# A pinned first tile with zero products beside it, and token sums moved into attention

## The chip, the cores and the metric

The kernel runs on one core of a Trainium2 chip. The metric is the device time of one execution in microseconds (us). The engines are TensorE (PE in the profile; its weight loads are PEld), VectorE (DVE), ScalarE (ACT), GpSimd (POOL) and SyncE (SP), which issues most of the loads.

## The reference

One decoder layer on 512 tokens behind 16 learned meta tokens, D = 1024, all in float32:

```python
h  = concat(meta_tokens, x)                    # 528 x 1024
hn = rmsnorm(h, norm_mix_pre)
rq, rk, rv, rg, sq, sk, sv, ga, gb = split(hn @ w_in)
y_ret = (silu(rg) * groupnorm(retention(rotary(rq), rotary(rk), rv))) @ w_ret_out   # 4 heads, dk 256, dv 512
y_sb  = stick_breaking(sq, sk, sv) @ w_sb_out                                      # 16 heads of 64
mix   = (sigmoid(ga) * y_ret + sigmoid(gb) * y_sb) @ w_out
h = h + rmsnorm(mix, norm_mix_post)
a, b = split(rmsnorm(h, norm_ffn_pre) @ w_ffn_in)                                  # 2816 each
h = h + rmsnorm((silu(a) * b) @ w_ffn_out, norm_ffn_post)
return h[16:]
```

## The kernel before

**Products in two parts.** Every float32 operand of a large product is split: ACT copies it to a rounded hi part (`wh`, `hT`, `th`), and VectorE subtracts that from the value for a lo part (`wl`, `hL`, `tl`); `split` and `lo_of` do this, at L104 and L101. A product is three passes, hi by hi, hi by lo and lo by hi (`mm`, L95). Transposes through TensorE are `turned`, L98.

**Weights** come as blocks of up to 1 MB into `raw` (two buffers), and are split into units of 1024 columns a partition (`wh`, `wl`, five buffers of each). A raw buffer is loaded again when its units are split, and a unit is written again when its products are done.

**Order.** The program is planned when it is built: a planner with a timeline of its own costs places the instructions of each engine, and may move an instruction past others where nothing forbids it. `keep_in_program_order` pins an instruction among the pinned ones. While `pinned[0]` is set, in attention and in the last products, all of PE's instructions are pinned. At run time each engine executes its queue in order.

**The stages that matter here, in order.**

1. The start. The gain `norm_mix_pre` (`grow`) is transposed and spread over a PSUM tile `gps`. The five tiles of the sequence (four of 128 tokens, `x0` to `x3`, and the meta tokens) are loaded, normalised (`innorm`: sum of squares on ACT at L666, the factor by `rstd_of` on VectorE and a power on POOL at L148, the scaled `hx` on VectorE at L671), transposed and split into `hT` and `hL`. Meanwhile the values of attention's first eight heads are formed (`Values(0)` and `Values(1)`, one weight block each, `part(j)` for token tile j), and then the first Q and K (`qk_work`), whose results take banks of `bank_p`, a pool of two.
2. Attention, eight pairs of heads. For each head, `head` lists scores (`z`: two sigmoids on ACT, a scan and a product on VectorE), transposes (`t`), the meta tokens' weights (`tm`, with copies on POOL) and the products with the values (`pv`); projections of the next pairs and of the branch gates fill in between as `Work` items.
3. The output projection of attention with `w_sb_out`, eight feature products of 5.6 us each.
4. Retention, head by head, beginning with `rv_proj(0)`: these projections use a seven-product scheme on quarters (`seven`, `tok_seven`), which needs sums of quarters of the weights (POOL, `tok_quarters`, L233 to L236 for the first block and L244 later) and of the tokens (`Tokens`: four sums for each of four feature tiles k, kept as `th` and `tl`).
5. The merge, the output projection, the FFN, and the last norm.

**Token sums.** `Tokens.row_steps(k, t, u)` is a generator. For one feature tile it issues ten pinned POOL operations of 256 columns (L175) into the four sums `t` with `u` as scratch, then a copy of all four to `th` on ACT (L184) and four pinned POOL subtractions into `tl`. Stage 3 calls it for all four tiles, eight steps beside each feature product:

```python
for _ in range(8):
    next(token_sums, None)
```

**The end.** For each token tile, two halves c of the last product are followed by a square with its sum on ACT (L1249), a product with the gain on VectorE (L1250), then the factor (`rs`, VectorE L1252 and a power on POOL L1253) and the last line on VectorE (L1256), whose result is stored.

Of the kernel before, what the change touches and what calls it, by code (L numbers as in the profile page):

```python
# [10 lines left out]
F32 = mybir.dt.float32  # L11
# [23 lines left out]
def hybrid_block(  # L35
# [64 lines left out]
    def lo_of(lo, src, hi):  # L100
        nc.vector.tensor_tensor(lo, src, hi.bitcast(F32), op=ALU.subtract)  # L101
# [51 lines left out]
    class Tokens:  # L153
# [15 lines left out]
        def row_steps(self, k, t, u):  # L169

            b11, b12, b21, b22 = [[v[:, k, :].bitcast(F32) for v in self.quarter(i, j)] for i in range(2) for j in range(2)]
            t1, t2, t3, t4 = [t[:, n, :] for n in range(4)]

            def op(d, p, q, o):
                tc.keep_in_program_order(nc.gpsimd.tensor_tensor(d, p, q, op=o))  # L175
# [8 lines left out]
            nc.scalar.activation(self.th[:, :, k, :], t, AF.Copy)  # L184
            for n in range(4):
                yield op(self.tl[:, n, k, :], t[:, n, :], self.th[:, n, k, :].bitcast(F32), ALU.subtract)
# [210 lines left out]
    with tc.tile_pool(name="s2", bufs=2, side=RS, reuse_waits="tile") as s2:  # L397
# [29 lines left out]
        class Values:  # L427
# [10 lines left out]

            def part(self, js):
# [47 lines left out]
        def qk_work(work, p, what="qk"):  # L487
# [3 lines left out]
            def q_steps(us):  # L491
                ps = bank_p()
# [12 lines left out]
            def k_steps(us):  # L505
# [3 lines left out]
                for i in range(2):  # L509
                    cs = slice(264 * i, 264 * (i + 1))  # L510
                    pk = bank_p()[:, :264]
# [118 lines left out]

        def tm(p, hd, j):
            turn_meta(hd, metas[p][hd])

# [25 lines left out]

        def innorm(i):  # L660
            n = NM if i == NT else P
            c0 = 0 if i == NT else NM + i * P
            xt = xts[i]
            junk = bank_a().rearrange("p a b -> p (a b)")
            ss = cst.tile([P, 1], F32, name=f"ss{i}")
            nc.scalar.activation(junk[:n], xt[:n], AF.Square, accum_out=ss[:n])  # L666
            rstd_of(ss[:n], ss[:n], 1e-6, 1.0 / D, n)
# [10 lines left out]
        nc.sync.dma_start(grow, g_mix_pre.rearrange("o (k p) -> (o k) p", p=P))  # L678
        xload(0)

        pg = bank_b()
        turned(pg[:, :KD], grow, ident[:KD, :KD])
        nc.scalar.activation(gcol, pg[:, :KD], AF.Copy)
        for k in range(KD):
            turned(gps[:, k // 4, (k % 4) * P : (k % 4 + 1) * P], gcol[:, k : k + 1].to_broadcast([P, P]), ident)
        vals = [Values(0), Values(1)]
        innorm(0)
        vals[0].load()
        xload(1)
# [82 lines left out]
    with tc.tile_pool(name="s3", bufs=1, side=RS, reuse_waits="tile") as s3:  # L772
        s3.tile([P, 2, T], F32, tag="gb", name="gb", bufs=2)

        def all_rows():
            for k in range(KH):
                t = s3.tile([P, 4, H], F32, tag="ts", name="ts", bufs=2)
                yield from tokens.row_steps(k, t, s3.tile([P, H], F32, tag="tu", name="tu", bufs=2))

        token_sums = all_rows()  # L780
# [12 lines left out]
        for f in range(0, KD, 2):  # L793
# [4 lines left out]
            for e in range(2):  # L798
# [4 lines left out]
                for _ in range(8):  # L803
                    next(token_sums, None)
# [398 lines left out]
    with tc.tile_pool(name="s8", bufs=2, side=RS, reuse_waits="tile") as s8:  # L1203
# [38 lines left out]
        for i in range(NT):  # L1242
            sc, fo = [col("sc0"), col("sc1")], s8.tile([P, D], F32, tag="fo", name="fo")
            for c in range(2):
# [4 lines left out]
                nc.scalar.activation(sq, banks[i][c], AF.Square, scale=D**-0.5, accum_out=sc[c])  # L1249
                nc.vector.tensor_tensor(fo[:, cs], banks[i][c], gfin[:, cs], op=ALU.mult)  # L1250
            rs = col("rs")
            nc.vector.scalar_tensor_tensor(rs, sc[0], 1e-6, sc[1], op0=ALU.add, op1=ALU.add)  # L1252
            nc.gpsimd.tensor_tensor(rs, rs, nhalf, op=ALU.pow)  # L1253
# [47 lines left out]
```

## Time and profile before

| | us |
|---|---|
| median of 3 runs | 1198.09 (1197.95 to 1198.48) |
| the profiled execution, its own time | 1197.83 |
| its span, first to last instruction | 1196.0 |
| TensorE busy | 1168.3 (98%) |
| VectorE busy | 851.2 (71%) |
| ScalarE busy | 529.8 (44%) |
| GpSimd busy | 348.7 (29%) |

In the rows of the profile, `out<-in` names the tiles of an instruction, a bracket at the end of a row tells how long its engine stood idle before it and what ended that, and L with a number is a line of the kernel. Rows of the timeline begin with the start and the duration in us; "x2" merges neighbouring instructions of a kind. Ends of products are modelled and overlap; the pitch from one start to the next is their rate.

### The profile page before, as it was taken

How to read it: one execution, taken by the hardware profiler on the slowest of the kernel's cores; microseconds unless marked ns; L12 is line 12 of the kernel's file. 1: busy time of each engine (PE TensorE's matmuls, PEld its weight loads, DVE VectorE, ACT ScalarE, POOL GpSimd, SP SyncE). 2: the span in 40 equal slices, each digit the busy share in tenths (PEclk: the TensorE clock that was granted, in tenths of full speed). 3: DMA queues.
4: the chain of work that ended last, by engine and by line, in shares of the span. 5: the costliest groups of instructions: out<-in, count | busy, mean ns of one | idle time of the engine just before them, and what ended most of it. 6: DMA issues, size and time to landing. Idle time of an engine off the chain costs nothing.

```text
span 1196.0 us, 18637 instructions
## 1 busy us (share of the span) xinstructions
PE 1168.3 (98%) x7521; PEld 1058.4 (88%) x7521; DVE 851.2 (71%) x1120; ACT 529.8 (44%) x899; POOL 348.7 (29%) x374
## 2 busy tenths in 40 slices
PE   7999999999999999999999999999999999999997
PEld 7988999988888988988898898788999999998886
DVE  5588788887447865687577657776799999983333
ACT  5476676666223434334243424344354444443321
POOL 2011122125864401340341120001366666620000
PEclk9999999999999999999999999999999999999999
DMA  6222222233532224122222414334132333253311
GB/s 196 84 85 89 63 64 73 75 99 110 190 116 71 81 71 141 36 81 100 78 73 79 141 54 141 132 135 139 44 106 81 114 98 130 84 185 106 103 39 71
DMA packets 98055, 118.24 MB, mean 99 GB/s; under 512 B 2584, under 2 KB 74272, under 8 KB 97968
## 3 DMA queue, kind: packets, MB, share of 16 engines
q1 hardware_dynamic: 97536, 115.98, 30.0%
q8 instruction: 59, 0.97, 0.3%
q10 hardware_dynamic: 432, 1.07, 0.3%
q14 instruction: 28, 0.23, 0.1%
HBM read 109.96 MB, written 7.08 MB: 98 GB/s over the span
## 4 chain that ended last, share of the span: by engine, by line
PE 76%; DVE 9%; POOL 6%; issue 4%; ACT 2%; DMA 2%; DVEq 0%; POOLq 0%; SPq 0%; ACTq 0%
PE pp L95 34%; PE pb L95 17%; PE pa L95 15%; PE pc L95 5%; DVE wl L101 3%; PE px L95 3%; PE pb L98 3%; DMA raw<-in_w_in_dram 2%; POOL ts L175 2%; POOL tl L175 2%; ACT wh L104 1%; DVE sm L574 1%; POOL raw L244 1%; POOL st L244 1%; DVE ub L266 1%
## 5 line engine op out<-in xcount | busy, mean ns | idle before, releaser
L101 DVE TENSOR_TENSOR wl<-raw,wh 128x1024 fp32r<-128x1024 f32 x196 | 265.9, 1363 | 79.5 <-ACT wh L104 76.1
L104 ACT ACTIVATE wh<-raw 128x1024 fp32r<-128x1024 f32 x196 | 196.9, 1013 | 209.0 <-PE pa L95 78.0
L95 PE MATMUL pp<-hT,wh 128*128 128x512 f32 (+1 forms) x320 | 116.5, 364 | 1.3 <-DVE qb L101 1.1
L95 PE MATMUL pp<-hL,wh 128*128 128x512 f32 (+1 forms) x320 | 112.3, 351 | 0.0
L95 PE MATMUL pp<-hT,wl 128*128 128x512 f32 (+1 forms) x320 | 112.1, 350 | 0.0
L101 DVE TENSOR_TENSOR wl<-st,wh 128x1024 fp32r<-128x1024 f32 x54 | 84.8, 1575 | 15.6 <-ACT wh L104 15.5
L244 POOL TENSOR_TENSOR st<-raw 128x512 f32<-128x512 f32 x28 | 43.6, 1579 | 159.8 <-DMA raw<-in_w_in_dram 159.8
L95 PE MATMUL pp<-qk,wh 128*128 128x512 f32 x256 | 83.2, 399 | 2.0 <-ACT qk L104 1.7
L95 PE MATMUL pp<-wh,hT 128*128 128x256 f32 (+1 forms) x240 | 75.0, 313 | 0.7 <-ACT hT L104 0.7
L95 PE MATMUL pp<-wh,hL 128*128 128x256 f32 (+1 forms) x240 | 74.4, 310 | 0.8 <-DVE ss L147 0.8
L95 PE MATMUL pp<-wl,hT 128*128 128x256 f32 (+1 forms) x240 | 73.9, 308 | 0.0
L104 ACT ACTIVATE wh<-st 128x1024 fp32r<-128x1024 f32 x54 | 56.0, 1055 | 35.5 <-POOL st L244 17.2
L95 PEld LDWEIGHTS pp<-hT,wl 128*128 128x128 f32 x320 | 60.2, 188 | 8.3
L584 POOL CAST mg<-sp 128x32 fp32r<-128x32 f32 x32 | 7.4, 230 | 204.5 <-DVE sp L575 155.1
L95 PEld LDWEIGHTS pp<-hT,wh 128*128 128x128 f32 x320 | 60.2, 188 | 7.5 <-issue 1.3
L95 PE MATMUL pa<-hT,wh 128*128 128x264 f32 (+1 forms) x192 | 62.4, 325 | 2.8 <-DVE rt L891 2.8
L95 PEld LDWEIGHTS pp<-hL,wh 128*128 128x128 f32 x320 | 60.4, 189 | 5.3
L574 DVE TENSOR_TENSOR_SCAN sm<-sm,mask 128x528 f32<-128x528 f32 (+1 forms) x64 | 54.9, 858 | 12.5 <-ACT sm L571 11.6
L148 POOL TENSOR_TENSOR rs<-rs,nhalf 128x1 f32<-128x1 f32 x20 | 12.7, 636 | 170.7 <-DVE rs L147 170.7
L95 PE MATMUL pa<-hL,wh 128*128 128x264 f32 (+1 forms) x192 | 62.2, 324 | 0.0
L95 PE MATMUL pa<-hT,wl 128*128 128x264 f32 (+1 forms) x192 | 62.1, 324 | 0.0
L95 PEld LDWEIGHTS pp<-qk,wh 128*128 128x128 f32 x256 | 47.6, 188 | 13.4 <-ACT qk L104 2.4
(326 smaller groups left out, 3726.8 us busy)
## 6 DMA issues: line engine op xcount, KB each, us to landing
raw<-in_w_in_dram SPq DMA_DIRECT2D x28, 1024.0 KB, 5.0
raw<-in_w_ffn_in_dram SPq DMA_DIRECT2D x22, 1024.0 KB, 5.1
raw<-in_w_in_dram SPq DMA_DIRECT2D x32, 512.0 KB, 4.2
raw<-in_w_ffn_out_dram SPq DMA_DIRECT2D x11, 1024.0 KB, 4.9
raw<-in_w_ret_out_dram SPq DMA_DIRECT2D x8, 1024.0 KB, 5.0
raw<-in_w_sb_out_dram SPq DMA_DIRECT2D x4, 1024.0 KB, 5.2
raw<-in_w_out_dram SPq DMA_DIRECT2D x4, 1024.0 KB, 5.0
ysb<-in_x_dram SPq DMA_DIRECT2D x4, 512.0 KB, 8.7
```

The source lines that it names most:

```text
L95: return keep(nc.tensor.matmul(*args, **kw))
L98: return keep(nc.tensor.transpose(dst, src, idn))
L101: nc.vector.tensor_tensor(lo, src, hi.bitcast(F32), op=ALU.subtract)
L104: ins = nc.scalar.activation(hi, src, AF.Copy)
L148: nc.gpsimd.tensor_tensor(dst, dst, nhalf[:n], op=ALU.pow)
L175: tc.keep_in_program_order(nc.gpsimd.tensor_tensor(d, p, q, op=o))
L244: nc.gpsimd.tensor_tensor(d[:, k : k + 2], p[:, k : k + 2], q[:, k : k + 2], op=op)
L266: nc.vector.tensor_tensor(ub[:, 1:4:2, :], p.rearrange("p (o n) -> p o n", o=1).to_broadcast([P, 2, n]), ub[:, 1:3, :], op=ALU.add)
L574: nc.vector.tensor_tensor_scan(rev, rev, mask[:, r0:][:, ::-1], 0.0, op0=ALU.mult, op1=ALU.max)
L584: nc.gpsimd.tensor_copy(g[:, two, 0:NM], m)
```

## The change

- The start. `grow` is loaded from ACT's queue, so x0's load is the first of SP's. The first value block is loaded as two halves (`Values.begin`), each split by `Values.take`. `first_tile` writes out the order of the first tile, pinned on ACT and VectorE: norm, hi of the first half block, both `hx`, transposes, lo of the first half block, hi and lo of both halves of the tile, then the second half block, then the norm of tile 1. The sum of squares of tile 0 is shared by ACT and VectorE. Five products of zeros stand ahead of the gain's transposes on PE and four behind them.
- The first K's two halves take banks of `bank_a` instead of `bank_p`.
- The token sums of feature tiles 0 and 1 are stepped in attention: six steps behind `turn_meta` of each head of the last two pairs. Their room is a buffer of the values' pool, their scratch one of the gates'. Tiles 2 and 3 stay in stage 3, four steps beside each feature product.
- All four lo parts of a tile's sums are one VectorE subtraction of 1024 columns instead of four POOL ones.
- In the last products the factor `rs` is issued ahead of the second half's product with the gain.

```diff
@@ row_steps
             nc.scalar.activation(self.th[:, :, k, :], t, AF.Copy)
-            for n in range(4):
-                yield op(self.tl[:, n, k, :], t[:, n, :], self.th[:, n, k, :].bitcast(F32), ALU.subtract)
+            yield lo_of(self.tl[:, :, k, :], t, self.th[:, :, k, :])
@@ Values
+            def begin(self):
...
+                for i in range(2):
+                    nc.sync.dma_start(self.raw[:, 4 * i : 4 * (i + 1)], src[:, 4 * i : 4 * (i + 1)])
+            def take(self, i):
+                raw = self.raw[:, 4 * i : 4 * (i + 1)]
+                u = [wun.tile([P, 4, 256], F32R, tag=n, name=n) for n in ("wh", "wl")]
+                self.units.append(u)
+                tc.keep_in_program_order(nc.scalar.activation(u[0], raw, AF.Copy))
+                return lambda: tc.keep_in_program_order(lo_of(u[1], raw, u[0]))
@@ tm
             turn_meta(hd, metas[p][hd])
+            if p == NPAIR - 2 and hd == 0:
+                room = s2.tile([P, 2, 4, H], F32, tag="vt", name="ts")
+                sums[0] = row_sums((0, 1), lambda k: (room[:, k], gate_tile()[:, :H]))
+            if p >= NPAIR - 2:
+                for _ in range(6):
+                    next(sums[0], None)
@@ the start
+        def norm(i):
...
+            if i == 0:
+                so = cst.tile([P, 1], F32, name="so")
+                jv = s2.tile([P, 512], F32, tag="qb", name="jv")
+                tc.keep_in_program_order(nc.scalar.activation(junk[:, 0:512], xt[:, 0:512], AF.Square, scale=D**-0.5, accum_out=ss))
+                nc.vector.scalar_tensor_tensor(jv, xt[:, 512:D], 1.0 / D, xt[:, 512:D], op0=ALU.mult, op1=ALU.mult, accum_out=so)
+                nc.vector.scalar_tensor_tensor(ss, ss, 1e-6, so, op0=ALU.add, op1=ALU.add)
+                nc.gpsimd.tensor_tensor(ss, ss, nhalf, op=ALU.pow)
+                return
...
+        def first_tile(v):
+            pin = tc.keep_in_program_order
+            norm(0)
+            los = [v.take(0)]
+            hxs, pts = [], []
+            for j in range(2):
+                hx = s2.tile([P, 512], F32, tag="qb", name="hx")
+                pin(nc.vector.scalar_tensor_tensor(hx, xts[0][:, 512 * j : 512 * (j + 1)], rss[0], gps[:, j, :], op0=ALU.mult, op1=ALU.mult))
+                hxs.append(hx)
+            for j in range(2):
+                pt = bank_b().rearrange("p (a b) -> p a b", a=4)
+                for a in range(4):
+                    turned(pt[:, a, :], hxs[j][:, a * P : (a + 1) * P], ident)
+                pts.append(pt)
+            los[0]()
+            for j in range(2):
+                ks = slice(4 * j, 4 * j + 4)
+                hi, lo = [v_[:, ks, NM : NM + P] for v_ in (hT, hL)]
+                pin(nc.scalar.activation(hi, pts[j], AF.Copy))
+                pin(lo_of(lo, pts[j], hi))
+            v.take(1)()
+            norm(1)
 
-        nc.sync.dma_start(grow, g_mix_pre.rearrange("o (k p) -> (o k) p", p=P))
+        nc.scalar.dma_start(grow, g_mix_pre.rearrange("o (k p) -> (o k) p", p=P))
         xload(0)
+        vals = [Values(0), Values(1)]
+        vals[0].begin()
+        xload(1)
+        zeros = s2.tile([P, T], F32R, tag="qa", name="zeros")
+        nc.vector.memset(zeros.bitcast(F32), 0.0)
+        idle = bank_p()
+        def idling(n):
+            for _ in range(n):
+                tc.keep_in_program_order(nc.tensor.matmul(idle, zeros[:, 0:P], zeros, start=True, stop=True))
+        idling(5)
...
+        idling(4)
+        first_tile(vals[0])
         vals[1].load()
         innorm(1)
         for i in range(2, NT + 1):
             xload(i)
+            norm(i)
...
+        def first_bank():
+            kp.append(None)
+            return bank_a()[:, 0, :] if len(kp) > 1 else bank_p()
-        qk_work(work, 0)
+        qk_work(work, 0, first_bank)
@@ stage 3
-                for _ in range(8):
+                for _ in range(4):
                     next(token_sums, None)
@@ the end
                 nc.scalar.activation(sq, banks[i][c], AF.Square, scale=D**-0.5, accum_out=sc[c])
+                if c:
+                    rs = col("rs")
+                    nc.vector.scalar_tensor_tensor(rs, sc[0], 1e-6, sc[1], op0=ALU.add, op1=ALU.add)
+                    nc.gpsimd.tensor_tensor(rs, rs, nhalf, op=ALU.pow)
                 nc.vector.tensor_tensor(fo[:, cs], banks[i][c], gfin[:, cs], op=ALU.mult)
-            rs = col("rs")
-            nc.vector.scalar_tensor_tensor(rs, sc[0], 1e-6, sc[1], op0=ALU.add, op1=ALU.add)
-            nc.gpsimd.tensor_tensor(rs, rs, nhalf, op=ALU.pow)
```

More of the change, by code (lines that the diff above doesn't have):

```diff
@@ L485, in hybrid_block, with qk_work @@
         flat = lambda t: t.rearrange("p a b -> p (a b)")
-        def qk_work(work, p, what="qk"):
+        def qk_work(work, p, bank=bank_p, what="qk"):
             def q_load():
@@ L662, in innorm @@
             c0 = 0 if i == NT else NM + i * P
[L663 to L667, printed above, removed]
+            xt, ss = xts[i], rss[i]
             for j in range(2):
@@ L773, in hybrid_block @@
         s3.tile([P, 2, T], F32, tag="gb", name="gb", bufs=2)
[L775 to L780, printed above, removed]
+        token_sums = row_sums((2, 3), lambda k: [s3.tile([P, n, H], F32, tag=t, name=t, bufs=2) for t, n in (("ts", 4), ("tu", 1))])
         yh = s3.tile([P, KD, T], F32R, name="yh")
```

31 lines of the change are left out of this document (23 added, 8 removed).

## The prediction

> **What bounds the kernel now.** I read the page first: the span and the busy line.
>
> ```profile
> span 1196.0 us, 18637 instructions
> ...
> PE 1168.3 (98%) x7521; PEld 1058.4 (88%) x7521; DVE 851.2 (71%) x1120; ACT 529.8 (44%) x899; POOL 348.7 (29%) x374
> ```
>
> TensorE (PE) is busy for 1168.3 of 1196.0 us. The change removes no product, so all it can win is PE's idle time, 27.7 us, and products that run slowly. Next came what PE waited for over the whole span (total, times, longest).
>
> ```profile
> PE pa L95 <- DVE rt L891: 2.8, 1, 2.8
> ...
> PE pb L98 <- DVE hx L671: 2.7, 1, 2.7
> ...
> PE pp L95 <- DVE qb L101: 1.1, 1, 1.1
> ...
> PE pa L95 <- DVE wl L101: 0.7, 1, 0.7
> ...
> PE pb L95 <- DVE wl L101: 0.6, 1, 0.6
> ```
>
> Then the stages, as busy time by window, to place these waits: the start, two pieces of attention, the sb output projection (291 to 336) and the first retention projection behind it. Columns: stage, its length, busy time (instructions) of PE, PEld, DVE, ACT, POOL, the clock, DMA share, GB/s.
>
> ```profile
> 0.00:18.10 18.10, 10.91 (x49) 9.73 (x50) 9.33 (x17) 11.99 (x19) 6.63 (x21) 1.00 0.84 269
> 18.10:41.10 23.00, 22.63 (x195) 22.29 (x193) 12.78 (x29) 7.14 (x16) 0.54 (x1) 1.00 0.15 44
> ```
>
> ```profile
> 235.00:262.00 27.00, 26.36 (x162) 23.35 (x161) 24.11 (x42) 19.91 (x49) 6.03 (x16) 1.00 0.38 118
> 262.00:291.00 29.00, 29.00 (x152) 24.34 (x151) 21.98 (x38) 16.94 (x39) 12.23 (x26) 1.00 0.20 68
> ```
>
> ```profile
> 291.00:336.00 45.00, 45.00 (x194) 36.19 (x193) 20.41 (x18) 12.66 (x13) 39.70 (x42) 1.00 0.48 162
> 336.00:383.00 47.00, 42.84 (x310) 40.08 (x308) 32.60 (x36) 17.65 (x24) 26.80 (x18) 1.00 0.36 119
> ```
>
> The reader is to see that the stage in which POOL is crowded, 291 to 336 (39.70 of 45), costs nothing itself: PE is busy for 45.00 of 45. Its price is paid in the next stage, where PE lacks 4.16 us. From 18.1 to 41.1 PE is the bound (22.63 of 23), so what the start wins is kept.
>
> **The start.** The first tile of x, in order of time:
>
> ```profile
> 0.73 0.39 SPq L678 DMA_DIRECT2D grow<-in_norm_mix_pre_dram  x1
> ...
> 5.10 1.03 ACT L666 ACTIVATE pa<-ysb 128x1024 f32<-128x1024 f32 x1 [1.90 <-DMA ysb<-in_x_dram]
> ...
> 7.11 1.41 DVE L671 SCALAR_TENSOR_TENSOR hx<-ysb,ss,pa 128x512 f32<-128x512 f32 x2 [0.67 <-POOL ss L148]
> ...
> 9.17 2.36 DVE L101 TENSOR_TENSOR wl<-raw,wh 128x1024 fp32r<-128x1024 f32 x2 [0.65 <-ACT wh L104]
> ...
> 12.57 0.41 PE L95 MATMUL pp<-wh,hT 128*128 128x256 f32 x1
> ...
> 12.78 0.41 PE L95 MATMUL pp<-wl,hT 128*128 128x256 f32 x1
> ...
> 14.18 2.35 DVE L101 TENSOR_TENSOR wl<-raw,wh 128x1024 fp32r<-128x1024 f32 x2
> ```
>
> ```profile
> 20.95 1.27 DVE L101 TENSOR_TENSOR hL<-pb,hT 128x512 fp32r<-128x512 f32 x2
> ...
> 22.35 0.28 PE L95 MATMUL pp<-wh,hT 128*128 128x256 f32 x1
> ...
> 22.47 0.28 PE L95 MATMUL pp<-wl,hT 128*128 128x256 f32 x1
> ```
>
> Two things lose time. VectorE does both weight splits (9.17, 2.36) ahead of the lo parts of the first tile, and the products run at a pitch of 0.21 (12.57 to 12.78) where later they take 0.12 (22.35 to 22.47). Now the new order, step by step. With grow's issue off SP (it goes to ACT's queue, where the table load is the only neighbour) x0 lands 0.39 earlier, at 4.7. The sum of squares is halved between ACT and DVE, saving some 0.4 of the 1.03. So hx runs from 6.3 to 7.7. On VectorE, now pinned, follow one split (1.18), two lo parts (0.64 each) and the other split (1.18): 8.9, 10.2, 11.4. The third product needs the first lo part, 9.6 instead of behind 9.17 + 2.36 and its lo part; the first twelve products at 0.12 reach 10.8, the other twelve follow the second split to 12.9. The second tile's hx (1.41, after its own power) ends by 13.8, the splits of the second value block (2.35) by 16.2, that tile's lo parts (1.27) by 17.5. The twelve products behind the last split end at 17.6, and the product that stood at 22.35 starts near 18.0, with four transposes ahead of it, 18.6. That is 3.75 earlier; I take **3.5**, since I gave VectorE no wait but one.
>
> The ends: if the planner keeps VectorE's order behind the first tile, only 0.8 and the wait of 0.65 at 9.17 go, 1.4. If the second tile's hx hides in VectorE's own wait, 4.5. The nine zero products go into PE's idle time (18.10 less 10.91). At the slow pitch a 512-column product is an estimate of 0.42, twice the row's 0.21 for 256; the last four could hold the transposes back by up to 0.7, inside the ends. Reading the weights as two half loads adds one SP issue of 0.4 ahead of x1, which has more than 3 us to spare. Whether the zeros raise the clock matters little to the sum: 24 products by 0.09 is 2.2 us of PE time, but the second value block's splits end at 16.2 either way, so at most 0.6 of it shows.
>
> **The first K projection.** Its second half stood 1.1 for qb, because three banks were asked of a pool of two; the change gives the K halves another pool. Nothing else is due there: **1.1**, between 0 (the weight split or a copy arrives last instead) and 1.1.
>
> **Token sums.** Rows of the two places they leave and enter:
>
> ```profile
> 280.01 0.73 POOL L175 TENSOR_TENSOR ts<-hT 128x256 f32<-128x256 f32 x1
> ```
>
> ```profile
> 246.57 1.26 DVE L574 TENSOR_TENSOR_SCAN sm<-sm,mask 128x528 f32<-128x528 f32 x1
> ...
> 261.49 1.22 DVE L101 TENSOR_TENSOR wl<-raw,wh 128x1024 fp32r<-128x1024 f32 x1
> ```
>
> ```profile
> 314.66 1.78 DVE L101 TENSOR_TENSOR wl<-raw,wh 128x1024 fp32r<-128x1024 f32 x1 [0.17 <-ACT wh L104]
> ...
> 325.91 1.23 DVE L101 TENSOR_TENSOR wl<-raw,wh 128x1024 fp32r<-128x1024 f32 x1
> ```
>
> Twenty POOL steps of 0.73 (14.6 us) move beside pairs 6 and 7, where POOL has 21 and 17 us free. Sixteen lo steps on POOL become four 1024-column subtractions on VectorE; two of them fall into attention. VectorE pays twice: 1.23 to 1.78 for each lo part, and a slowing of operations with two SBUF operands while POOL works (1.78 against 1.23, some 0.5). In the first piece of attention six such operations lie where the steps will run, the first at 246.57 and the last at 261.49: 3.0, and one lo part 1.7, against 2.9 free (27 less 24.11). In the second three: 1.5 and 1.7 against 7.0. PE's order is pinned there, so an excess stalls it: 0 to 1.8. I take **+1.0**, the middle, since PE already lacks 0.64 in that first piece. The temporaries are buffers of finished values and of the gates; they come free before the steps.
>
> What it buys, at 336 to 383:
>
> ```profile
> 346.84 2.93 POOL L236 TENSOR_TENSOR raw<-raw 128x1024 f32<-128x1024 f32 x1
> ```
>
> ```profile
> 347.44 2.41 DVE L838 TENSOR_TENSOR xd<-hL 128x64 f32<-128x64 f32 x1
> ```
>
> ```profile
> 349.80 3.21 SPq L112 DMA_DIRECT2D raw<-in_w_in_dram  x2
> ```
>
> ```profile
> 364.62 2.33 DVE L101 TENSOR_TENSOR wl<-raw,wh 128x1024 fp32r<-128x1024 f32 x1
> ```
>
> ```profile
> 372.16 3.53 POOL L244 TENSOR_TENSOR raw<-raw 128x512 f32<-128x512 f32 x2 [4.07 <-DVE rvm L101]
> ```
>
> ```profile
> 382.99 0.59 PE L95 MATMUL pa<-hT,wh 128*128 128x264 f32 x1 [2.81 <-DVE rt L891]
> ```
>
> POOL ends the last weight sum at 349.77. VectorE's 64-column xd stands beside it for 2.41 us, the load of the next weights starts only at 349.80, the split of the K weights (364.62) runs 2.33 beside POOL, and the sums for the gate weights start at 372.16, ending in the 2.81 us stall at 382.99. The other two tiles' steps, four beside each feature product, are all issued by the sixth of eight products; with half the steps gone and the lo parts off POOL, it is through by about 337, and the two waits for wl (0.7 and 0.6) go: 1.3. Of the 2.81 the chain through POOL gets back 1.1 from the uncontended split alone and up to all of it from the earlier load; I take 2.0. Sum **3.3**, ends 1.3 and 4.1. Late next are the same engines for the gate's sums, but they move with PE, since the K weights wait for units that PE frees.
>
> **The end.** The last tile:
>
> ```profile
> 1190.15 0.69 DVE L1250 TENSOR_TENSOR fo<-pc,gfin 128x512 f32<-128x512 f32 x1 [2.00 <-ACT sq L1249]
> 1190.76 0.15 DVE L1252 SCALAR_TENSOR_TENSOR rs<-sc,sc 128x1 f32<-128x1 f32 x1
> 1190.99 0.55 POOL L1253 TENSOR_TENSOR rs<-rs,nhalf 128x1 f32<-128x1 f32 x1 [4.89 <-DVE rs L1252]
> 1191.57 1.41 DVE L1256 SCALAR_TENSOR_TENSOR fo<-fo,rs,h 128x512 f32<-128x512 f32 x2 [0.66 <-POOL rs L1253]
> ```
>
> With rs first, at 1190.15, the power runs beside the product with gfin, and the last line starts at 1190.96: **0.6**, between 0.5 and 0.7.
>
> **The sum**: -3.5 - 1.1 + 1.0 - 3.3 - 0.6 = -7.5. The profiled execution took 1197.83 (span 1196.0 and 1.83 around it), 0.26 under the median of 1198.09; so 1190.3 by its own time and 1190.6 against the median.
>
> **Rivals.** First, VectorE keeps its old order at the start: 1.4 for 3.5, 1192.7. For it: VectorE is nearly full from 9 to 16.5. Against: the second tile's transposes now come before the splits are through. Second, the stall at 382.99 stays and only 1.3 is won there: 1192.6; the planner decides whose split goes first. Third, beside POOL each VectorE operation with two SBUF operands loses a whole POOL step, 0.73 rather than 0.5: six and the lo part make 6.3 in the first piece against 2.9 free, +3.4 for +1.0, 1193.0.
>
> The Trainium skill has this rule in "SBUF — State Buffer", section "Who interferes with whom": an operation with two SBUF inputs contends with a GpSimd operation that reads SBUF, and the loser blocks fully. By it the sum would be -5.1, by the row -7.5; the trace shows 1.78 for 1.23, less than a whole step, so I hold to the row.
>
> Fourth, slower than before: ACT and VectorE work in order, and th (ACT) with its lo part (VectorE) may be queued before POOL has done the tenth step.
>
> ```profile
> ACT th L184 <- POOL ts L175: 13.9, 1, 13.9
> ```
>
> That is ACT standing 13.9 us for just this, though with nothing urgent behind it. In attention the score sigmoids and scans are behind it. Four steps late (2.9), th (about 1.03) and the lo part (1.78) make 5.7 a sum, 11.4 for two: 10.4 over my +1.0, 1201.0. It decides from 4.3 us a sum. Against it: the planner orders by its own times for POOL, and ten steps span two heads. Fifth, the planner leaves the steps where they were and the start stays VectorE's: 1.1 + 0.6 + 0.4 are won, 1196.0.
>
> **How the numbers follow.** Forecast 0.50 (alone, 1188 to 1193), first 0.14, second 0.11, third 0.10, fourth 0.07, fifth 0.08. A measurement of this kernel tells 0.2% (2.4 us) from no change; the fifth lies inside it, so faster 0.85, same 0.08, slower 0.07. All good ends together give -10.4, 1187.7; above, the range takes in the first three rivals with some of their own spread: 1187.5 to 1195.5.
>
> **What would show it.** Right: products at a 0.12 pitch before 13 us and VectorE's first hL before 10; no wait for qb near 50; POOL's L175 steps from 245 on and its last weight sum by about 340; no wait for wl or rt before 380; L1253 ahead of L1250's end. Wrong: ACT's th waiting for POOL between 240 and 285 with PE idle beside it, PE's idle time in pair 6 above 2 us, or the second tile's products still starting behind 20.

## The result, and the profile after

The changed kernel took 1191.94 us (median of five, 1191.47 to 1193.73) against 1198.23 for the kernel before (five, 1197.95 to 1200.78): ratio 0.9942, 95% interval [0.9931, 0.9954]. That is 6.3 us less where 7.5 were forecast. The page, span and busy time:

```profile
span 1189.9 us, 18649 instructions
...
PE 1167.4 (98%) x7530; PEld 1055.7 (89%) x7530; DVE 858.8 (72%) x1127; ACT 529.8 (45%) x899; POOL 343.0 (29%) x358
```

TensorE (PE) did the same work and nine products of zeros more, so the 6.1 us of the span came out of its idle and slow time. What it waited for now (total, times, longest):

```profile
PE pb L95 <- DVE ub L265: 3.5, 3, 1.4
PE pb L98 <- DVE al L101: 2.9, 2, 1.8
PE px L95 <- DVE al L101: 2.7, 4, 1.6
PE pp L95 <- ACT qk L104: 1.7, 3, 0.6
PE pp L760 <- DVE zeros L755: 1.5, 1, 1.5
PE pp L95 <- DVE gb L884: 0.9, 1, 0.9
```

The waits for rt (2.8), hx (2.7), qb (1.1) and wl (0.7 and 0.6) are off the list. The waits for al, PE's operand in attention, have grown (before they were 1.1 and 0.8 in total), and the one for gb in stage 3 is new.

To see where the time went I took, from the views of single tiles, the start of PE's first or last product of each stage. The table gives the length of each stretch between such marks: from 0 to the first "v-tail" product (values of the meta tokens, reads xmd); to the first score (px from ka, qa); to the first value product (px from ah, vt); the last pair (the last px from ka, qa, a score of that pair's first head, to the last px from al, vt, its last value product); stage 3 (first product that reads yh to first that reads xm); transition (from there to the first pp from qk). The other stretches differ by under 0.8 in these two kernels. Each figure is from one profile: kernels with the same start have their v-tails between 37.1 and 37.8, so a difference of some tenths in one stretch is not told from chance.

| kernel (profiled run) | v-tails | score | value | last pair | stage 3 | transition |
|---|---|---|---|---|---|---|
| before | 41.1 | 21.4 | 18.9 | 19.8 | 50.7 | 100.5 |
| after | 37.2 | 20.6 | 20.2 | 22.9 | 51.5 | 94.1 |
| difference | -3.9 | -0.8 | +1.3 | +3.1 | +0.8 | -6.4 |

Two stretches won more than forecast, three gave some back. **The start** went nearly step by step as written. Timeline of after, in order of start:

```profile
6.44 1.41 DVE L732 SCALAR_TENSOR_TENSOR hx<-ysb,ss,pa 128x512 f32<-128x512 f32 x2 [1.00 <-PE pa L98]
7.76 1.22 DVE L101 TENSOR_TENSOR wl<-raw,wh 128x1024 fp32r<-128x1024 f32 x1
...
8.90 1.28 DVE L101 TENSOR_TENSOR hL<-pb,hT 128x512 fp32r<-128x512 f32 x2
...
9.64 0.38 PE L95 MATMUL pp<-wh,hL 128*128 128x256 f32 x1 [0.22 <-DVE hL L101]
9.86 0.27 PE L95 MATMUL pp<-wh,hT 128*128 128x256 f32 x1
9.97 0.28 PE L95 MATMUL pp<-wl,hT 128*128 128x256 f32 x1
...
10.17 1.23 DVE L101 TENSOR_TENSOR wl<-raw,wh 128x1024 fp32r<-128x1024 f32 x1
```

The lo parts (8.90) stand between the two weight splits (7.76 and 10.17), the third product starts at 9.64, and the pitch is 0.11 to 0.12 from there, where it was 0.21 at 12.57.

**What the start gave back** shows on ScalarE at the first sigmoid, after and then before:

```profile
58.33 1.28 ACT L587 ACT_TABLE_LOAD   x1 [1.60 <-PE px L95]
59.62 0.39 ACT L587 ACTIVATE sm<-px 128x264 f32<-128x264 f32 x1
```

```profile
61.01 1.28 ACT L571 ACT_TABLE_LOAD   x1
62.98 0.39 ACT L571 ACTIVATE sm<-px 128x264 f32<-128x264 f32 x1 [0.69 <-PE px L95]
```

Before, the load ran ahead of the scores (62.5) and cost nothing; after, ScalarE first waits for them (57.8), then loads. 1.3 of the 4.7 won so far is lost.

**Attention** is paid for by VectorE. Windows of the last two pairs, before and then after:

```profile
229.00:256.00 27.00, 26.36 (x178) 24.05 (x177) 23.86 (x41) 20.04 (x49) 5.65 (x15) 1.00 0.28 84
256.00:284.00 28.00, 28.00 (x153) 23.66 (x152) 20.73 (x37) 15.65 (x39) 10.12 (x28) 1.00 0.30 103
```

```profile
229.00:256.00 27.00, 25.91 (x165) 23.11 (x163) 25.04 (x41) 19.47 (x48) 10.97 (x20) 1.00 0.34 106
256.00:284.00 28.00, 25.83 (x136) 20.99 (x135) 23.31 (x33) 15.96 (x38) 23.46 (x34) 1.00 0.23 78
```

POOL rises from 10.12 to 23.46 in the second window and PE falls from 28.00 to 25.83: the loss is in pair 7, not in pair 6, whose VectorE had looked the fuller one. There ScalarE's copy th stood 2.66 us for POOL, and PE waited twice behind it, 0.30 and 1.58:

```profile
262.66 1.06 ACT L184 ACTIVATE th<-ts 128x1024 fp32r<-128x1024 f32 x1 [2.66 <-POOL ts L175]
...
264.26 0.49 PE L95 MATMUL px<-ah,vt 128*128 128x512 f32 x1 [0.30 <-ACT ah L104]
...
264.45 1.23 DVE L101 TENSOR_TENSOR tl<-ts,th 128x1024 fp32r<-128x1024 f32 x1
...
266.33 0.50 PE L95 MATMUL px<-al,vt 128*128 128x512 f32 x1 [1.58 <-DVE al L101]
```

The longer of the two is the lo part's doing as well: ah was ready at 264.20, but VectorE ran tl first and began al, for which PE waited, at 265.60. ACT's th waiting for POOL with PE idle beside it is one of the prediction's own signs of being wrong.

**The transition**, POOL's last weight sum, the load of the next weights, and xd:

```profile
335.64 2.43 POOL L235 TENSOR_TENSOR raw<-raw 128x1024 f32<-128x1024 f32 x1
...
340.35 0.38 SPq L112 DMA_DIRECT2D raw<-in_w_in_dram  x1
...
341.44 0.20 DVE L921 TENSOR_TENSOR xd<-hL 128x64 f32<-128x64 f32 x1
```

POOL is done at 338.07 instead of 349.77, xd takes 0.20 instead of 2.41, the load is issued at 340.35 instead of 349.80, and between 340 and 390 PE waits for nothing.

**The end**, the last tile:

```profile
1184.55 0.16 DVE L1335 SCALAR_TENSOR_TENSOR rs<-sc,sc 128x1 f32<-128x1 f32 x1 [2.03 <-ACT sq L1332]
1184.62 0.68 DVE L1337 TENSOR_TENSOR fo<-pc,gfin 128x512 f32<-128x512 f32 x1
1184.79 0.55 POOL L1336 TENSOR_TENSOR rs<-rs,nhalf 128x1 f32<-128x1 f32 x1 [4.89 <-DVE rs L1335]
1185.37 1.41 DVE L1340 SCALAR_TENSOR_TENSOR fo<-fo,rs,h 128x512 f32<-128x512 f32 x2
```

From the start of the last product (1183.34) to the last line 2.03, where it was 2.63 (1188.94 to 1191.57): 0.6.

### The profile page after: what moved, and what is told of

Read it like the earlier page. It is cut to its first block, busy times and chain, and to the rows that moved or that the text cites. A ratio compares the mean times of both kernels' runs of the same rounds, so it can differ in the third digit from the quotient of the medians.

```text
span 1189.9 us, 18649 instructions
## 1 busy us (share of the span) xinstructions
PE 1167.4 (98%) x7530; PEld 1055.7 (89%) x7530; DVE 858.8 (72%) x1127; ACT 529.8 (45%) x899; POOL 343.0 (29%) x358
## 4 chain that ended last, share of the span: by engine, by line
PE 82%; DVE 10%; issue 2%; ACT 2%; DMA 2%; POOL 2%; DVEq 0%; POOLq 0%; ACTq 0%; SPq 0%
PE pp L95 37%; PE pb L95 18%; PE pa L95 17%; PE pc L95 5%; DVE wl L101 3%; PE px L95 3%; PE pb L98 2%; DMA raw<-in_w_in_dram 2%; DVE sm L590 2%; ACT wh L104 1%; POOL raw L243 1%; DVE al L101 1%; POOL st L243 1%; DVE yl L101 1%; DVE sp L591 1%
## 5 line engine op out<-in xcount | busy, mean ns | idle before, releaser
L95 PE MATMUL pp<-hT,wh 128*128 128x512 f32 (+1 forms) x304 | 112.0, 368 | 0.2 <-ACT ga L1133 0.2
L95 PE MATMUL pp<-hL,wh 128*128 128x512 f32 (+1 forms) x304 | 107.7, 354 | 0.0
L95 PE MATMUL pp<-hT,wl 128*128 128x512 f32 (+1 forms) x304 | 107.6, 354 | 0.0
L95 PE MATMUL pa<-hL,wh 128*128 128x264 f32 (+1 forms) x208 | 66.2, 318 | 0.0
L95 PE MATMUL pa<-hT,wh 128*128 128x264 f32 (+1 forms) x208 | 66.2, 318 | 0.0
L95 PE MATMUL pa<-hT,wl 128*128 128x264 f32 (+1 forms) x208 | 66.1, 318 | 0.0
L95 PEld LDWEIGHTS pp<-hT,wl 128*128 128x128 f32 x304 | 57.2, 188 | 8.3
L95 PEld LDWEIGHTS pp<-hT,wh 128*128 128x128 f32 x304 | 57.3, 188 | 6.0 <-ACT ga L1133 0.5
L95 PEld LDWEIGHTS pp<-hL,wh 128*128 128x128 f32 x304 | 57.4, 189 | 5.3
```

The lines of the kernel that those rows point to most:

```text
L95: return keep(nc.tensor.matmul(*args, **kw))
```

## The experiments

My theory: the start wins its 4 us wherever the sums stand; the transition is won by relieving POOL; attention pays for the place of the sums. The rival: one of the three does not act alone. The kernels were timed in three groups (e1 to e4, e5 to e8, e9 to e12), each beside its own runs of the kernel before (1198.72, 1198.08 and 1198.85 us), so kernels of different groups are compared by their ratios. Stretches are those of the table above.

**e1, the start alone.** Of the change only the first tile's order, the zeros and the first K bank; the sums, their lo parts and the end as before:

```
+        token_sums = all_rows()            # all four tiles in stage 3, eight steps a product
-            yield lo_of(self.tl[:, :, k, :], t, self.th[:, :, k, :])
+            for n in range(4):              # POOL again
+                yield op(self.tl[:, n, k, :], ...)
```

> The start (pinned first tile, zero products, half loads, the K bank) alone; token sums, their lo parts and the last tile as before. Account by stages: 4.7 us won at the first score, 1.3 given back there because the sigmoid's table load on ACT now waits for the score, nothing else lost in attention: 1194.8 (3.4 under before), PE's lead at the first product of the sb output projection still 3.2 to 3.4, and the 2.8 us stall behind rv_proj as before. Rival, that attention eats any lead PE arrives with: 1197 to 1198, lead at that product under 1.

Measured: 1194.08, ratio 0.9963 [0.9949, 0.9977], 4.4 us by the ratio. The v-tails came at 37.1, the last pair took 19.9, stage 3 50.3 and the transition 100.3, as before: the start acts alone. PE's lead at the first product of stage 3 was 1.4 for the expected 3.2 to 3.4. But the stretch to the first value product was 21.8, not 20.2 as in after, at the same 1.8 us wait. The windows say why, this kernel and then after (the column behind the five engines is the granted clock):

```profile
70.00:75.00 5.00, 3.19 (x24) 2.98 (x24) 4.88 (x9) 3.18 (x9) 0.85 (x3) 0.93 0.38 108
75.00:80.00 5.00, 5.00 (x25) 4.52 (x23) 4.73 (x8) 3.33 (x8) 0.52 (x2) 0.73 0.00 0
```

```profile
70.00:75.00 5.00, 3.19 (x27) 2.98 (x26) 4.88 (x9) 2.90 (x8) 0.57 (x2) 1.00 0.38 108
75.00:80.00 5.00, 5.00 (x29) 4.31 (x28) 4.91 (x10) 3.92 (x9) 0.52 (x2) 1.00 0.00 0
```

Behind a wait of 1.8 us PE's clock fell for a while, in one profile and not in the other. The loss is 5.00 x (0.07 + 0.27) = 1.7 us, and most of what the lead lacks.

**e2, the sums alone.** Token sums and lo parts as in after; start, K bank and end as before:

```
+            if p >= NPAIR - 2:
+                for _ in range(6):
+                    next(sums[0], None)
-                for _ in range(8):
+                for _ in range(4):
                     next(token_sums, None)
```

> The token sums alone: tiles 0 and 1 beside pairs 6 and 7, all lo parts on VectorE; start and end as before. Account by stages: attention's last pairs lose 3.1 and the sb output projection 0.9, the stage behind it wins 6.4 (4.2 idle, the rest products at half rate behind the stall): 1195.8, first sb product about 3 us later than before. Rival, that the loss in the last pairs belongs to the lead from the start: no loss there, 1191.8.

Measured: 1197.28, ratio 0.9992 [0.9982, 1.0002]: next to nothing. The transition shrank to 94.1 all the same, so 6.4 us were won and 4.8 lost again: the last pair 23.8 (+4.0, with a stretch of low clock at 271 in it), stage 3 51.5 (+0.8). It had two such stretches in its profile (at 271 and 527), the kernel before one. The moved sums are worth little as they stand, about 1 us where the account by stages gave 2.9, which I had not forecast.

**e3, all sums in stage 3.** After, but nothing beside attention; the lo parts stay on VectorE:

```
-        token_sums = row_sums((2, 3), ...)
+        token_sums = row_sums((0, 1, 2, 3), ...)
-                for _ in range(4):
+                for _ in range(8):
```

> The changed kernel, but all four tiles' sums stay beside the sb output projection, eight steps a product, lo parts on VectorE. If moving the lo parts off POOL is what frees the stage behind it: attention's loss of 3.1 goes and the 6.4 stay, 1188.8, with the last weight sum of the first V block by 345. Rival, halving POOL's steps there is what frees it: the stall of 2.8 and the slow products behind it come back, 1193 to 1195.

Measured: 1188.64, ratio 0.9922 [0.9909, 0.9935], some 2.4 us better than after by the ratios. The last pair is back at 19.9, the transition stays at 94.2. Sixteen POOL steps given to VectorE free POOL by themselves; moving two tiles' sums beside attention only cost. The price is stage 3, 51.8.

**e4, no zeros.** After without the nine idle products:

```
-        idling(5)
-        idling(4)
```

> The changed kernel without the nine zero products. If the splits on VectorE set the pace of the start, as in the prediction: first products at a pitch of 0.21, but at most 0.6 us later at the second tile, 1191.9 to 1192.5. Rival, the clock sets it: 24 and more products at half rate, 2.2 us and more, 1194.1 or later.

Measured: 1195.90, ratio 0.9981 [0.9970, 0.9992], 4.7 us worse than after by the ratios, far from the "at most 0.6". In the profile the products start at a pitch of 0.22 (until 11.6) and the first score comes 1.3 later (59.1 for 57.8). Another part goes with the clock: its twelve runs had a mean granted clock of 0.9960 against 0.9980 of after's five, which by 1194 us is 2.4 us; its profile shows two stretches of low clock, at 268 and 524. That makes 3.7 of the 4.7; 1.0 stays open. Leaving out products at 1.5 and 6 us shifts where later waits fall, and the last section shows that a wait's place decides whether the clock falls; why more of these runs should have met it, they do not say. The rival's time came in, but its own term, the slow first products, is the 1.3.

**e5, the stall of before filled.** The kernel before, with sixteen products of 512 columns into a spare bank, never read, in the 2.81 us stall at 382.99:

```
             pk = bank_a()
+            if h == 0 and e == 1:
+                fill = bank_b()
+                for _ in range(16):
+                    nc.tensor.matmul(fill, hT[:, 0, NM : NM + P], xtok(0), start=True, stop=True)
```

> The kernel before, with sixteen products of 512 columns (0.22 us each, 3.5 us) into a spare PSUM bank, never read, ahead of the first retention head's second K projection, where TensorE stood 2.81 us at 382.99 and then ran thirteen or so products at a pitch of 0.22 instead of 0.12. The planner moves the eleven gate products that stood ahead of that stall behind it (11 x 0.12 = +1.3), so that about 0.9 us of standing is left. Theory (the stall takes TensorE's clock down to half for some 3.4 us, 1.7 us a time): no product of 264 columns at a pitch of 0.22 behind 383, granted clock 1.00 there, and -1.7 + 1.3 = -0.4, about 1198.3. Rival (the slow products have another cause, their operands or the weight loads): the pitch of 0.22 stays and the eleven gate products are simply added, about 1200.

Measured: 1195.03, ratio 0.9974 [0.9963, 0.9984]: useless products made the kernel before 3.1 us faster. Windows before, then filled:

```profile
380.00:385.00 5.00, 2.19 (x11) 2.02 (x10) 4.96 (x7) 2.21 (x3) 1.66 (x1) 0.78 0.00 0
385.00:390.00 5.00, 5.00 (x38) 5.00 (x38) 1.55 (x2) 0.00 (x0) 0.00 (x0) 0.88 0.00 0
```

```profile
380.00:385.00 5.00, 5.00 (x30) 4.21 (x29) 4.96 (x7) 2.21 (x3) 1.46 (x1) 1.00 0.00 0
385.00:390.00 5.00, 5.00 (x44) 5.00 (x43) 2.33 (x4) 1.06 (x1) 0.00 (x0) 1.00 0.02 3
```

The 264-column products behind the stall start 0.12 apart instead of 0.22, and seven of the eight runs had a granted clock of 0.999, where the runs of before in the same group had 0.996 to 0.998. The stall itself made the slow products: 5.00 x (0.22 + 0.12) = 1.7 us. My sum was too small in one term: I had charged 1.3 for the eleven gate products pushed behind the stall, but PE's next waits (1.1 for ub, 0.6 for qk) are both gone between 370 and 480, so it seems that they went into these.

**e6, the table early.** After, with a sigmoid of one column behind the first Q's evacuation:

```
                 nc.scalar.activation(qb[64:128], ps[64:128], AF.Copy)
+                if p == 0:
+                    dm = cst.tile([P, 1], F32, name="dm")
+                    nc.scalar.activation(dm[64:128], qb[64:128, 0:1].bitcast(F32), AF.Sigmoid)
```

> The kernel after, with one sigmoid of one column right behind the first Q's evacuation on ScalarE (about 48.9), so that the load of the sigmoid table (1.28 us at 58.33, between the first scores and their sigmoid) falls where ScalarE stood idle. Theory (that load is what took 1.3 us of the start's gain back at the first scan): first sigmoid at 58.3, first scan 1.3 earlier, the wait for the transposed scores at 72.6 down from 1.8 to 0.5 or so; about 1190.6, ratio 0.9935 to the kernel before. Rival (TensorE has other work there, the load is hidden, and the start's gain went in the projections' order): 1191.7 to 1192.0.

Measured: 1191.96, ratio 0.9946 [0.9934, 0.9959], no gain. Locally it did what the theory said:

```profile
50.32 1.28 ACT L516 ACT_TABLE_LOAD   x1
...
58.99 0.39 ACT L590 ACTIVATE sm<-px 128x264 f32<-128x264 f32 x1 [1.62 <-PE px L95]
```

The stretch to the first value product is 19.0 for 20.2 and the wait at 72.6 is 0.46 for 1.81. In this profile 0.6 of that was lost to a later start (v-tails at 37.8) and the rest behind 830, where no new wait is named. The theory of the place holds, that of the whole does not.

**e7, th later.** After, with th two turns of the generator later and pinned, and the steps drained behind the last pair:

```
+            for _ in range(2):
+                yield
-            nc.scalar.activation(self.th[:, :, k, :], t, AF.Copy)
+            th = nc.scalar.activation(self.th[:, :, k, :], t, AF.Copy)
+            if k < 2:
+                tc.keep_in_program_order(th)
```

> The kernel after, with the copies of the token sums to their hi part on ScalarE two turns of the generator later and pinned, so that none stands in ScalarE's queue ahead of pair 7's attention with its POOL step still to come. Theory (ScalarE, queued 2.66 us behind that copy, held up the ah and al of pair 7): the TensorE waits of 0.30 and 1.58 at 264 to 266 go, the last value product of pair 7 comes at about 282 instead of 284.5; 1189.4 to 1190.2. Rival (the loss in pair 7 is VectorE beside POOL, each operation slower, whatever ScalarE's queue does): pair 7 still ends at 284 or later, 1191.4 to 1192.

Measured: 1193.48, ratio 0.9960 [0.9948, 0.9973], slower than after. The waits of 0.30 and 1.58 shrank to one of 0.44, but one of 1.42 for al came at 278 instead, the last pair took 22.3, and stage 3 grew to 53.0 with a wait of 1.7 for gb. Moving th won 0.6 of the 3.1 in the last pair and put another wait in the place of the old ones, so the run does not tell how much ScalarE's queue costs by itself; by the total the rival was nearer.

**e8, lo parts on POOL.** After, the four subtractions on POOL again, the sums' places kept (the steps drained behind the last pair):

```
-            yield lo_of(self.tl[:, :, k, :], t, self.th[:, :, k, :])
+            for n in range(4):
+                yield op(self.tl[:, n, k, :], t[:, n, :], self.th[:, n, k, :].bitcast(F32), ALU.subtract)
```

> The kernel after, with the four subtractions of each token sum's lo part on POOL again (eight tiles' quarters beside attention, eight in stage 3, 0.74 us or more each), the sums of the first two tiles still beside attention. If moving two tiles out of stage 3 is enough to free POOL for the weight sums: their last is done by about 347 instead of 338, no stall of TensorE between 380 and 390, and the time is 1191.5 to 1193.5. If the lo parts were what held POOL: the weight sums end behind 350, the stall before 390 is back, 1194.5 to 1197.

Measured: 1190.30, ratio 0.9938 [0.9926, 0.9951], by the medians better than after, by the intervals not told apart. The transition is 94.0 again: freeing POOL in either way is enough. The last pair took 21.9 and stage 3 50.5, and PE waits for nothing in stage 3: in after the lo parts on VectorE cost about 1.0 in each of the two places.

**e9, e3 and e6 together.** All sums in stage 3, and the table early:

```
-        token_sums = row_sums((2, 3), ...)
+        token_sums = row_sums((0, 1, 2, 3), ...)
...
+                    nc.scalar.activation(dm[64:128], qb[64:128, 0:1].bitcast(F32), AF.Sigmoid)
```

> All four feature tiles' token sums in stage 3, their lo parts on VectorE, and the table of the sigmoid loaded early: the two experiments together. If the stretches of the profile add up (first score to first value product 19.0 instead of 20.3, the last pair's stretch 19.9, the transition 94.2): 1188.6 - 1.3 = 1187.3, ratio 0.991 to the kernel before. Rival (what the table's load gives is given back at the next wait for the transposed scores, as the whole time of the early table alone suggested): 1188.6.

Measured: 1189.20, ratio 0.9921 [0.9909, 0.9933], the same as e3: the rival came in. The stretches are as expected (19.0, 19.8, 94.1), and the first pp from qk comes 1.5 earlier than in e3 (432.6 for 434.1), but the stretch from there to the last pp from qk took 356.5 for 355.4 and the one behind 830, from the first product of the FFN (reads nT) to the first that reads gh, 230.2 for 229.4. That stretch is 230.1 to 230.2 in all three kernels with the early table (e6, e9, e10) and at most 229.7 in the other eleven, so some 0.5 is lost there each time; why, no run shows.

**e10, the lo parts divided.** As e9, with the lo parts of the last two tiles on POOL:

```
+            if k < 2:
                 yield lo_of(self.tl[:, :, k, :], t, self.th[:, :, k, :])
+            else:
+                for n in range(4):
+                    yield op(self.tl[:, n, k, :], ..., ALU.subtract)
```

> As the kernel with all sums in stage 3 and the table loaded early, but the lo parts of the last two tiles on POOL in four pieces, of the first two on VectorE. Theory (one half freed is enough, and each lo part on VectorE beside POOL costs stage 3 some 0.4): POOL has 8 x 0.74 = 5.9 us more to do than with all four lo parts on VectorE, its weight sums end some 6 us later, behind 340 but ahead of the transition's need, stage 3 (first product of its output projection to the next) shrinks from 51.8 to about 51, the transition stays at 94 to 94.5; 1186.6 to 1187.3. Rival (with all sums in stage 3 POOL has no 6 us to spare): the transition grows to 96 to 100, 1189 to 1193.

Measured: 1187.37 (1186.88 to 1187.89), ratio 0.9905 [0.9891, 0.9918], the best of all. POOL's last weight sum:

```profile
335.51 2.41 POOL L239 TENSOR_TENSOR raw<-raw 128x1024 f32<-128x1024 f32 x1
```

It ends at 337.9, no later than in after, where the transition is 94.1; and stage 3 is 50.5. Both prices are gone: nothing stands beside attention, and in stage 3 PE waits for nothing, where in e9, with four lo parts on VectorE, it stood 1.1 for wh.

**e11, one tile.** After, one tile's sums beside the last two pairs, three steps a call, three tiles in stage 3:

```
-                sums[0] = row_sums((0, 1), ...)
+                sums[0] = row_sums((0,), ...)
-                for _ in range(6):
+                for _ in range(3):
                     next(sums[0], None)
-        token_sums = row_sums((2, 3), ...)
+        token_sums = row_sums((1, 2, 3), ...)
-                for _ in range(4):
+                for _ in range(6):
                     next(token_sums, None)
```

> The kernel after with one tile's sums beside the last two pairs instead of two, three POOL steps a call instead of six; the other three tiles in stage 3, lo parts on VectorE. Theory (the stretch of the last pair is lengthened by VectorE running slower beside POOL and by the steps queued there, so by the number of steps): from the last score's first product to the last value product 22.9 falls to about 21.4, half of the way to 19.9; transition still 94; stage 3 about 51.6; 1190.0 to 1190.6. Rival (one collision, whatever the number of steps): the stretch stays above 22.3, 1191.5.

Measured: 1190.35, ratio 0.9932 [0.9917, 0.9947]. The last pair took 21.2: 19.8 without, 21.2 with one tile, 22.9 with two. The steps are not alone in this: 0.8 of the 1.4 is PE's wait for al, which VectorE began behind the one lo part (282.71 to 284.47). Stage 3 took 50.3 instead of the 51.6 expected, without a wait, with three lo parts on VectorE. VectorE's scans of 400 columns (all on SBUF, four in the window 229 to 284) follow the number of tiles: the groups of e3, of this kernel, and of after:

```profile
L590 DVE TENSOR_TENSOR_SCAN sm<-sm,mask 128x400 f32<-128x400 f32 x4 | 3.9, 985 | 0.0
```

```profile
L590 DVE TENSOR_TENSOR_SCAN sm<-sm,mask 128x400 f32<-128x400 f32 x4 | 4.5, 1119 | 0.0
```

```profile
L590 DVE TENSOR_TENSOR_SCAN sm<-sm,mask 128x400 f32<-128x400 f32 x4 | 5.5, 1368 | 0.0
```

985, 1119, 1368 ns, and in e8, without lo parts on VectorE, still 1365: POOL's steps slow them. The scans of 528 columns do not follow it, 1258, 1378 and 1392: one tile slows them nearly as much as two.

**e12, the old K bank.** After, the first K projection's banks as before:

```
-        qk_work(work, 0, first_bank)
+        qk_work(work, 0)
```

> The kernel after, with the first K projection's PSUM banks handed out as before the change. Theory: TensorE waits some 1.1 us for the evacuation of the first Q's bank again, the stretch from the first v-tail product to the first score is 21.4 to 21.7 instead of 20.6, and with nothing behind that would take it up the time is 1192.7 to 1193.0. Rival (other products fill that wait): stretch 20.6 to 20.9, 1191.9.

Measured: 1192.48, ratio 0.9948 [0.9934, 0.9961], about 0.7 worse than after by the ratios, inside the intervals. PE's waits between 37 and 62:

```profile
PE pp L95 <- DVE kl L101: 1.4, 1, 1.4
PE pp L95 <- DVE qb L101: 0.9, 1, 0.9
```

The stretch to the first score is 22.7, 2.1 longer; but the table load is then hidden again and the next stretch is 18.9 for 20.2. Net 0.8: what the bank wins, the table load takes back in part.

## Why the prediction was right, and where its sizes were not

- **The start, -3.5: right.** -3.9 in the profiles compared; 37.1 to 38.0 in all eleven kernels that have the new order, 41.1 to 41.9 in the three that have the old. The first rival (VectorE keeps its order) did not come about.
- **The zeros, at most 0.6: wrong.** The argument followed the second value block's splits and looked no further than the v-tails, where it was nearly right (0.8). It left out the clock: 1.3 at the first score, and 4.7 for the whole kernel, of which about half goes with the lower granted clock (e4). The traces' record of the clock has its first full stretch from 17.55 in the kernel before, where the pitch turns from 0.21 to 0.12, from 11.72 in e4 and from 6.09 in after. Nothing is recorded ahead of that, so the clock of 1.00 in the prediction's row for 0 to 18.1 is no reading.
- **The first K projection, -1.1: right in mechanism.** The wait for qb is gone; 0.8 in the profile, 0.7 or so for the whole (e12, inside the intervals). I had written "Nothing else is due there"; what was due next was an activation table load of 1.28, hidden only because the scores came late.
- **Attention, +1.0: the term that was mis-sized.** It cost 3.1 in the last pair. The runs divide it in two: the lo part on VectorE is about 1.0 (e8 against after), and about 2.0 comes with POOL's steps and the copy th beside attention (e8's 21.9 against e3's 19.9). They do not divide the second part. th waiting for POOL, my fourth rival, came about once, at 2.66 us instead of the 5.7 I had priced, but e7, which moved it, put another wait in its place; POOL's steps slow VectorE (e8, e11), but I could not take the slowing away by itself. I counted VectorE's free time per window, seven us in the second piece. PE's order is pinned, and the wait of 1.58 hung on VectorE's queue between the last scores and the next value product, so the free time there is what I should have counted; no run tests that count. Another 0.8 went in stage 3, where I had priced the lo parts at nothing. It is one wait behind a lo part beside POOL, and its place decides, not the number of lo parts, since e11 has three there and no wait:

```profile
300.82 1.76 DVE L101 TENSOR_TENSOR tl<-ts,th 128x1024 fp32r<-128x1024 f32 x1
...
303.45 0.48 PE L95 MATMUL pp<-yh,wh 128*128 128x512 f32 x1 [0.95 <-DVE gb L884]
```

- **The third rival's rule.** Rows of after in pair 7, VectorE and POOL side by side:

```profile
258.48 1.09 POOL L175 TENSOR_TENSOR ts<-ts,hL 128x256 f32<-128x256 f32 x1
258.89 1.76 DVE L101 TENSOR_TENSOR wl<-raw,wh 128x1024 fp32r<-128x1024 f32 x1
259.65 1.60 POOL L175 TENSOR_TENSOR ts<-hT,ts 128x256 f32<-128x256 f32 x1
260.58 1.52 DVE L590 TENSOR_TENSOR_SCAN sm<-sm,mask 128x400 f32<-128x400 f32 x1
```

VectorE lost 0.53 twice (1.23 to 1.76, 0.99 to 1.52), as I had taken it, not a whole POOL step of 0.73; but POOL's step took 1.60 instead of 0.73. Both sides pay, and I had priced POOL's twenty steps at 0.73 each. Each of the last three begins while the other engine's operation runs; what was left of that is 0.68, 1.00 and 0.67 by these rows, and the losses are 0.53, 0.87 and 0.53. So one waits for about the rest of the other, which is less than a whole step for VectorE and more than one for POOL. The Trainium skill ("SBUF — State Buffer", section "Who interferes with whom") calls the ports that the two share "an exclusive lock"; these rows agree with it to some 0.15 us. What the third rival would make of the time, +3.4, came near the measured 3.1, but by luck: it had the loss in pair 6, and it was in pair 7.
- **The transition, -3.3: right in mechanism, half the size.** All three waits went, 0.7 + 0.6 + 2.8, where I gave the last one 2.0. The other 1.7 is the slow products behind the stall, which I had not read: the rows at a 0.22 pitch behind 382.99 were there to be seen, beside a clock of 0.78 in that window (e5 shows that the stall causes them). That makes 5.8 of 6.4; 0.6 stays unassigned. And the reason I gave was one too many: lo parts on VectorE alone (e3) or two tiles moved alone (e8) bring the same 94.
- **The end, -0.6: right**, by the rows of the last tile; no run has it alone.

The differences have opposite signs: the transition 3.1 and the start 0.4 better than forecast, attention 2.1, stage 3 0.8, the table load 1.3 and the K bank 0.3 worse, net 1.0 of the 1.2 by which the sum was off. That it came out so near is partly luck.

## What to carry to other kernels

When an engine is relieved, relieve it in the cheapest way that suffices: here either half of the edit freed POOL, and the half that put its work beside a pinned, nearly full VectorE cost more than it brought. Price a stall of TensorE with the slow products behind it, and if it can't be removed, fill it, even with products that nobody reads. When a stage starts earlier, look for what its lateness was hiding, such as a table load.

## What the runs showed of the hardware

TensorE's clock falls behind stalls much shorter than I had thought. In the profiles it fell behind waits of 2.8 (before), 2.4 and 1.8 (e1) and 1.8 (e11), behind the waits of pair 7 (e2, e4, e12) and in the retention stage (e2, e4, e8). Each of these ten stretches is 3.41 us long in the trace's record of the clock, at 0.50, which is the same 1.7 us each time. The 1.8 us wait near 72 left the clock alone in after, e3, e4, e7 and e8.

The record shows what tells them apart. In e1 the clock changed at 6.06, 74.33, 77.74, 381.53 and 384.94, which is 20, 1, 89 and 1 times 3.413 us from one to the next; the changes lie on such a grid in every profile, with a start of its own in each. Windows of this grid around the wait near 72, in e1 and then in after (the first figure behind the length is PE's busy time):

```profile
70.92:74.33 3.41, 1.60 (x14) 1.44 (x13) 3.33 (x7) 2.08 (x6) 0.02 (x1) 1.00 0.55 157
74.33:77.74 3.41, 3.41 (x16) 3.31 (x15) 3.35 (x7) 1.35 (x3) 0.26 (x1) 0.50 0.00 0
```

```profile
70.95:74.36 3.41, 1.75 (x15) 1.76 (x16) 3.31 (x7) 1.98 (x6) 0.00 (x0) 1.00 0.52 147
```

In e1 the whole wait lies in one window; in after it begins 0.15 ahead of one. Over the fourteen profiles the ten falls come behind windows in which PE was busy for 0.82 to 1.66 us, and no window with 1.75 or more was followed by one; e3's window at 70.99, with 1.59, is the only exception. So what counts is the idle time in one window; half of it, 1.7 us, is an estimate from these figures of what is enough. It is read off the traces, with one exception, and not tested: no run here moved a wait within its window on purpose.

The Trainium skill ("TensorE: Matmul & The Clock Gate", section "Part 1: The HAM clock gate (the "warmup" mystery)") says that the clock halves after an idle window of about 3.4 us and that this window runs freely, not from the kernel's start. The grid and the length of the slow stretch agree with that; that a wait of 1.8 us, not 3.4, can be enough does not. It is also why single runs of one kernel differ: the 23 of before beside e1 to e4 had a granted clock of 0.994 to 0.999 and took 1196.1 to 1201.5 us, about 1 us for each 0.001.
